# Sums for the down products on GpSimd's queue, a buffer of its own for the mean's weights, six places for the weight halves

## The chip, the cores and the metric

The kernel runs on one core of a Trainium2 chip. The metric is the device time of one execution in microseconds. Before the change it is 1877.29 us, the median of three runs (1876.36 to 1880.88).

## The reference

One layer of a decoder trunk is computed for a prompt of 1024 tokens and for eight sample tokens, 1032 columns in all, at a width of 1024, in float32. A combined projection feeds three branches (a gated linear recurrence, attention in a sliding window, attention into a memory of 256 tokens). Their outputs are gated, merged and projected, and then come a layer norm, a gated feed-forward part of width 2816 and a second layer norm:

```python
h = layer_norm(ALPHA * x + merged @ w_out, ln1_g, ln1_b)
gt, up = jnp.split(h @ w_gate_up, 2, axis=-1)
h = layer_norm(ALPHA * h + (jax.nn.silu(gt) * up) @ w_down, ln2_g, ln2_b)
```

The change bears on the feed-forward part: `h @ w_gate_up` (44 tiles of 128 output rows) and the product with `w_down` (8 tiles of 128 output rows over 22 tiles of input).

## The kernel before, in words

All data lie with the 128 rows of a tile on the partitions and the 1032 columns in the free dimension. A matrix product in float32 is made of three products in a rounded format: each operand is cut into a high half, written by ScalarE (L84), and a low half, the remainder, written by VectorE (L85), and the products high times high, high times low and low times high are summed in a bank of PSUM (matmuls in L332 to L334).

The large products save matmuls with seven products in place of eight for a two by two block scheme (Strassen's scheme in Winograd's form). A unit is a pair of weight tiles; step `i` of a unit (0 to 6) multiplies a weight block, or a sum of blocks, with a block or a sum of blocks of the columns. `fast_quarter` forms what a step needs of the weights: for some steps a sum by VectorE (L306), then the two halves. `fast_step` issues its 24 matmuls and takes the result out of PSUM.

The gate/up stage (`gate_up_down`, about 1230 to 1630 us in the trace) runs twenty gate/up units, of which eighteen go in nine pairs `u`, `v`; in a pair some of the products are themselves split again by the same scheme (steps named `p0` to `p6` and `v0` to `v6`, formed in `second_quarter` and `fifth_quarter`, run in `second_step` with matmuls in L1525 to L1527 and in `fifth_step` with L1465 to L1467). Eight units of the down product follow. The list `order` holds all steps. At each step the loop forms the weights of the step that is `ahead` = 3 places later, and then issues the step itself.

The weight halves have their places in `half_pair`: five for high halves (tag `qh`) and, in this stage, five for low halves (four with tag `ql` in one pool, every fifth in another). A half may be written when the matmuls that read its place's last content are done.

In step 0 of `v`, VectorE adds a bank of the split product (`pd`) to a partial sum (L389 in `fast_step`). The second product written to that bank, by the matmul at L1525 in step `p4`, has to wait for this reading.

For the down product the column operands are blocks of the gated activations, spilled to `scr_f` in HBM by `FinishGate` (L2059), and four sums of such blocks. `down_sums` forms the sums ahead of time, once for each of the two parts of the down product and twice in each part (`p` = 0, 1): three blocks are loaded (L1548 in `down_block`, 516 KB each), two differences are taken (L1563, L1565) and stored to `scr_t` (L1558 in `keep`), a fourth block is loaded and two more sums are formed and stored (L1570, L1573). All these DMAs are issued from SyncE's queue, which also issues the loads of raw weights (L265), the operands of the split products (L1417) and the spills. The blocks lie in z slots: eight buffers of 1032 columns, handed out in turn (`zt`) and given back (`zfree`), that the results of the units use too.

`weight_means` forms, for the mean of the second layer norm, the sums of the last six input tiles of `w_down`: eight loads of 384 KB (L1775) into a z slot, each followed by a reduction on VectorE (L1777), one load or reduction at every step 0 and 4.

Within the queues of the engines a planner orders the instructions by the order in which the program lists them and by the times at which it expects their inputs; an instruction that waits holds up all those behind it in its queue. Pools of SBUF memory are opened and closed by stage. `cst` and `sm` stay open to the end.

Of the kernel before, what the change touches and what calls it, by code (L numbers as in the profile page):

```python
# [19 lines left out]
P = 128  # L20
D = 1024
KT = D // P
TP = 1024
NB = 8
# [16 lines left out]
QN = T // 4  # L41
# [19 lines left out]
class Builder:  # L61
# [338 lines left out]
    def project(self, ctx, pool):  # L400

        nc, io, tc = self.nc, self.io, self.tc
        self.qdc = self.cst.tile([P, KT * NB], F32, name="qdc")
        self.qds = self.cst.tile([P, KT * NB], F32, name="qds")
        self.kd = self.cst.tile([P, 2 * NB], F32, name="kd")
        self.vd = self.cst.tile([NB, 256], F32, name="vd")
# [15 lines left out]
        ahead = 3  # L422
# [219 lines left out]
    def mem_scores(self, h, half, q, mk, between):  # L642

        nc = self.nc
        out = []
        for pr in range(2):
            s = self.bank("s", f"cs{h}_{half}_{pr}")
            for u in range(2):
                qt = pr * 2 + u
                self.mm3(s[:, u * 256:(u + 1) * 256], [  # L650
                    ((q[j][0][:, qt * P:(qt + 1) * P], q[j][1][:, qt * P:(qt + 1) * P]), mk[j]) for j in range(2)
                ])
            st = self.sm.tile([P, 8], F32, tag="cst", name=f"cst{h}_{half}_{pr}", bufs=4)
            p = self.ph.tile([P, 4 * 129], F32, tag="p", name=f"cp{h}_{half}_{pr}", bufs=4)[:, :512]
            nc.vector.tensor_reduce(st[:, 0:2], s.rearrange("p (a b) -> p a b", b=256), axis=AX.X,
                                    op=ALU.max, negate=True)
            for u in range(2):
                nc.scalar.activation(p[:, u * 256:(u + 1) * 256], s[:, u * 256:(u + 1) * 256], AF.Exp,
                                     bias=st[:, u:u + 1], scale=1.0, accum_out=st[:, 2 + u:3 + u])
            nc.vector.reciprocal(st[:, 4:6], st[:, 2:4])  # L660
            for u in range(2):
                nc.vector.tensor_scalar_mul(p[:, u * 256:(u + 1) * 256], p[:, u * 256:(u + 1) * 256],
                                            st[:, 4 + u:5 + u])
            out.append(p)
            if pr == 0:
                between()
        return out
# [108 lines left out]
    def win_scores(self, kv, ops, b, between=lambda: None):  # L776
# [7 lines left out]
        st = self.sm.tile([P, 12], F32, tag="bst", name=f"bst{kv}_{b}", bufs=4)  # L784
# [127 lines left out]
    def lru_consts(self):  # L912
# [3 lines left out]
        w = self.cst.tile([P, 8 * KT], F32, name="lruc")  # L916
# [3 lines left out]
        self.nsnk = self.cst.tile([P, 16], F32, name="nsnk")  # L920
        nc.vector.tensor_scalar_mul(self.nsnk, self.vec[:, V_SNK:V_SNK + 16], -1.0)
        self.hbg = self.cst.tile([P, 24], F32, name="hbg")
# [18 lines left out]
        self.sp4n = self.cst.tile([P, KT], F32, name="sp4n")  # L941
        nc.vector.tensor_scalar_mul(self.sp4n, t, -4.0)

    def lru_setup(self):
        self.scv = self.cst.tile([P, KT, 3, NB], F32, name="scv")
        self.scvo = self.cst.tile([P, KT, 3, NB], F32, name="scvo")
        self.sh = self.cst.tile([P, KT, NB], F32, name="sh")
        self.sho = self.cst.tile([P, KT, NB], F32, name="sho")
        self.pconv = self.cst.tile([P, KT, 3], F32, name="pconv")
        self.pho = self.cst.tile([P, KT], F32, name="pho")  # L950
# [84 lines left out]
    def dec_rows(self, qd, m0, dr, name):  # L1035

        nc = self.nc
        rows = self.sm.tile([NB, 256], F32, tag="drow", name=f"drow_{name}{m0}", bufs=1)
        ps = self.bank("o", f"drt_{name}{m0}")
        for i in range(2):  # L1040
            nc.tensor.transpose(ps[:NB, i * P:(i + 1) * P], qd[:, (m0 + i) * NB:(m0 + i + 1) * NB], self.ident)
        nc.scalar.copy(rows, ps[:NB, :256])
        nc.sync.dma_start(dr, rows)

    def dec_mem(self, h):
# [46 lines left out]
        st = self.sm.tile([P, 8], F32, tag="cst", name=f"dcst{h}", bufs=4)  # L1092
# [32 lines left out]
    def dec_win(self):  # L1125
# [9 lines left out]
        work = self.sm.tile([P, 256], F32, tag="drow", name="dwork", bufs=1)  # L1135
# [31 lines left out]
        st = self.sm.tile([P, 8], F32, tag="cst", name="dsst", bufs=4)  # L1167
# [10 lines left out]
        own = self.sm.tile([P, 8], F32, tag="cst", name="down", bufs=4)  # L1178
# [365 lines left out]
    def down_block(self, part, kh, th, p):  # L1544

        t = self.zt(f"f{part}{kh}{th}{p}")
        f0, t0 = 8 * part + 4 * kh, HT * th + QN * p
        self.nc.sync.dma_start(t.rearrange("p (k n) -> p k n", k=4), self.scr["f"][:, f0:f0 + 4, t0:t0 + QN])  # L1548
        return t

    def down_sums(self, part):


        tt = self.nc.vector.tensor_tensor
        for p in range(2):

            def keep(i, t):
                self.nc.sync.dma_start(self.scr["t"][:, part, p, (1, 2, 4, 6).index(i), :], t)  # L1558
# [4 lines left out]
            tt(b22, b22, b12, ALU.subtract)  # L1563
            keep(4, b22)
            tt(b12, b11, b12, ALU.subtract)  # L1565
# [34 lines left out]
    def gate_up_down(self, ts):  # L1600
# [29 lines left out]
        ahead = 3  # L1630
# [137 lines left out]
    def weight_means(self):  # L1768
# [3 lines left out]
        for m in range(KT):  # L1772
            z = self.zt(f"wsum{m}")
            raw = z[:, :nf * P]
            nc.sync.dma_start(raw, self.io["wdn"][m][:, f0 * P:(f0 + nf) * P])  # L1775
            yield
            nc.vector.tensor_reduce(part[:, m, :], raw.rearrange("p (k n) -> p k n", k=nf), axis=AX.X, op=ALU.add)  # L1777
            self.zfree(z)
            yield
# [183 lines left out]
    def build(self):  # L1963
# [8 lines left out]
        self.cdec = self.cst.tile([P, KT, NB], F32, name="cdec")  # L1972
# [12 lines left out]
        with ExitStack() as right:  # L1985
            slots = right.enter_context(ExitStack())
            self.slots = [slots.enter_context(pool("slots0", "right"))]
            with pool("acc") as acc, pool("gp") as self.gp:
# [23 lines left out]
                with pool("slots1") as slots1:  # L2012
# [212 lines left out]
```

## Time and profile before

| | |
|---|---|
| time, median of 3 runs | 1877.29 us (1876.36 to 1880.88) |
| time of the profiled execution | 1878.54 us |
| span of its instructions | 1876.8 us |
| TensorE (PE) busy | 1857.2 us, 99% of the span |
| VectorE (DVE) busy | 1441.6 us, 77% |
| ScalarE (ACT) busy | 1055.0 us, 56% |
| GpSimd (POOL) busy | 123.3 us, 7% |
| moved by DMA | 326.93 MB, 174 GB/s on average |

An instruction's row in a timeline gives its start and its duration in us, the engine, the line of the kernel, the operation, what it writes and reads by the program's names, and in brackets how long the engine was idle before it and what ended that. SP is SyncE; SPq rows are DMAs that it issues. A row of a line's instructions gives the shortest, median and longest duration in ns and the first and last start. Rows of waits give who waited for whom, the total in us, how many times and the longest.

### The profile page before, as it was taken

The page shows a single profiled execution, that of the slowest core. Times are in us where ns is not written, and L with a number is a line of the kernel's source. Part 1 is how long each engine was busy: PE and PEld are TensorE (multiplying, and loading weights), DVE is VectorE, ACT ScalarE, POOL GpSimd, SP SyncE. Part 2 cuts the span into 40 slices and gives each one's busy share as a digit, 9 for nine tenths or more (in the row PEclk, how much of TensorE's full clock was granted, in tenths as well). Part 3 has the DMA queues.
Part 4 walks back from the last instruction along what each step waited for, and adds up shares of the span by engine and source line. Part 5 has one row for each costly group of instructions (what it writes and reads, how often), then busy time and mean ns, then how long its engine had stood idle before and what let it go on. Part 6 is the DMA issues. An engine that isn't in the chain of part 4 may idle for free. (4 is left out here: it accounts for less than half of the span.)

```text
span 1876.8 us, 38124 instructions
## 1 busy us (share of the span) xinstructions
PE 1857.2 (99%) x14616; PEld 1839.9 (98%) x14616; DVE 1441.6 (77%) x2932; ACT 1055.0 (56%) x2250; POOL 123.3 (7%) x187
## 2 busy tenths in 40 slices
PE   9999999999999999999999999999999999999998
PEld 9999999999999999999999999999999999999998
DVE  7878878888789757568787567798787787857486
ACT  6576676665666756568774234544444434735355
POOL 1000002110000000021210000000000000001100
PEclk9999999999999999999999999999999999999999
DMA  9535345447344358647536251245586467866962
GB/s 337 171 115 175 110 143 168 137 139 263 119 160 168 121 195 272 212 128 238 173 99 190 91 192 57 69 167 183 183 272 205 154 216 246 262 169 188 206 184 91
DMA packets 186678, 326.93 MB, mean 174 GB/s; under 512 B 19760, under 2 KB 97536, under 8 KB 186496
## 3 DMA queue, kind: packets, MB, share of 16 engines
q1 hardware_dynamic: 179392, 304.86, 49.2%
q0 software_dynamic: 4224, 14.78, 3.9%
q10 hardware_dynamic: 2880, 4.85, 0.7%
q8 instruction: 115, 1.88, 0.4%
q14 instruction: 67, 0.55, 0.1%
HBM read 238.76 MB, written 89.84 MB: 175 GB/s over the span
## 5 line engine op out<-in xcount | busy, mean ns | idle before, releaser
L332 PE MATMUL ub<-th,u_6h 128*128 128x258 f32 x240 | 68.5, 285 | 1.3 <-DVE zb L380 0.6
L332 PE MATMUL ub<-th,u_2h 128*128 128x258 f32 x240 | 68.2, 284 | 0.9 <-ACT p1s L373 0.9
L332 PE MATMUL uc<-th,u_3h 128*128 128x258 f32 x240 | 68.1, 284 | 0.5 <-ACT v L503 0.5
L332 PE MATMUL ub<-th,u_4h 128*128 128x258 f32 x240 | 68.2, 284 | 0.2 <-ACT u2s L373 0.2
L332 PE MATMUL ud<-th,u_1h 128*128 128x258 f32 x240 | 68.1, 284 | 0.0
L334 PE MATMUL ud<-th,u_5l 128*128 128x258 f32 x240 | 68.1, 284 | 0.0
L332 PE MATMUL ud<-th,u_5h 128*128 128x258 f32 x240 | 68.1, 284 | 0.0
L332 PE MATMUL ub<-th,u_0h 128*128 128x258 f32 x240 | 68.1, 284 | 0.0
L334 PE MATMUL ub<-th,u_6l 128*128 128x258 f32 x240 | 68.1, 284 | 0.0
L334 PE MATMUL ub<-th,u_0l 128*128 128x258 f32 x240 | 68.1, 284 | 0.0
L334 PE MATMUL ud<-th,u_1l 128*128 128x258 f32 x240 | 68.1, 284 | 0.0
L334 PE MATMUL ub<-th,u_4l 128*128 128x258 f32 x240 | 68.1, 284 | 0.0
L334 PE MATMUL ub<-th,u_2l 128*128 128x258 f32 x240 | 68.1, 284 | 0.0
L334 PE MATMUL uc<-th,u_3l 128*128 128x258 f32 x240 | 68.0, 283 | 0.0
L333 PE MATMUL ub<-tl,u_6h 128*128 128x258 f32 x240 | 67.7, 282 | 0.0
L333 PE MATMUL ub<-tl,u_0h 128*128 128x258 f32 x240 | 67.7, 282 | 0.0
L333 PE MATMUL ud<-tl,u_5h 128*128 128x258 f32 x240 | 67.6, 282 | 0.0
L333 PE MATMUL ub<-tl,u_4h 128*128 128x258 f32 x240 | 67.6, 282 | 0.0
L333 PE MATMUL ud<-tl,u_1h 128*128 128x258 f32 x240 | 67.6, 282 | 0.0
L333 PE MATMUL ub<-tl,u_2h 128*128 128x258 f32 x240 | 67.6, 282 | 0.0
L333 PE MATMUL uc<-tl,u_3h 128*128 128x258 f32 x240 | 67.6, 282 | 0.0
L134 PE MATMUL op<-mh,woh 128*128 128x258 f32 x224 | 63.4, 283 | 0.0
(1080 smaller groups left out, 8228.8 us busy)
## 6 DMA issues: line engine op xcount, KB each, us to landing
ur<-win SPq DMA_DIRECT2D x120, 256.0 KB, 3.1
raw<-wgu SPq DMA_DIRECT2D x80, 256.0 KB, 3.5
t<-scr_t SPq DMA_DIRECT2D x36, 516.0 KB, 4.8
z<-scr_f SPq DMA_DIRECT2D x28, 516.0 KB, 4.8
scr_f<-z SPq DMA_DIRECT2D x22, 516.0 KB, 2.8
scr_t<-z SPq DMA_DIRECT2D x20, 516.0 KB, 3.2
raw<-wdn SPq DMA_DIRECT2D x35, 256.0 KB, 4.7
z<-scr_t SPq DMA_DIRECT2D x16, 516.0 KB, 8.8
```

Source lines behind the costliest of these rows:

```text
L134: nc.tensor.matmul(ps, sh, mh, start=opens and i == 0, stop=False)
L332: mm(sh[:, w], xh, start=opens and k == 0, stop=False)
L333: mm(sh[:, w], xl, start=False, stop=False)
L334: self.last_mm = mm(sl[:, w], xh, start=False, stop=k == 3).ins
```

## The change

The diff makes five edits.

- In the gate/up and down stage, high and low halves have six places each instead of five. The added places lie in the pool `w1`.
- The weights of a step are formed four steps ahead instead of three.
- In `down_sums` the loads of the blocks and the stores of the sums are issued from GpSimd's queue instead of SyncE's.
- `weight_means` loads into a buffer of its own in `w1` instead of a z slot, in sixteen pieces of 192 KB instead of eight of 384 KB, with sixteen reductions.
- Small tiles that only the first stages use (states, softmax columns and the like) move from `cst` and `sm` to a new pool `early`, which is closed before the pool `zf` of the out projection and the gate/up stage is opened. This gives the memory for the places and the buffer. No instruction on these tiles changes.

```diff
     def half_pair(self, name):
-        low = partial(self.wpool.tile, tag="ql", bufs=4)
+        high, low = (partial(self.wpool.tile, tag=f"q{e}", bufs=n) for e, n in (("h", 5), ("l", 4)))
         if self.sfree is not None:
             self.lows += 1
-            if self.lows % 5 == 0:
-                low = partial(self.w1.tile, tag="ql", bufs=1)
-        return self.wpool.tile([P, D // 2], F32R, tag="qh", name=f"{name}h", bufs=5), low([P, D // 2], F32R, name=f"{name}l")
+            if self.lows % 6 > 3:
+                low = partial(self.w1.tile, tag="ql", bufs=2)
+            if self.lows % 6 == 5:
+                high = partial(self.w1.tile, tag="qh", bufs=1)
+        return high([P, D // 2], F32R, name=f"{name}h"), low([P, D // 2], F32R, name=f"{name}l")
...
-    def down_block(self, part, kh, th, p):
+    def down_block(self, part, kh, th, p, queue=None):
...
-        self.nc.sync.dma_start(t.rearrange("p (k n) -> p k n", k=4), self.scr["f"][:, f0:f0 + 4, t0:t0 + QN])
+        (queue or self.nc.sync).dma_start(t.rearrange("p (k n) -> p k n", k=4), self.scr["f"][:, f0:f0 + 4, t0:t0 + QN])
...
     def down_sums(self, part):
-        tt = self.nc.vector.tensor_tensor
+        tt, other = self.nc.vector.tensor_tensor, self.nc.gpsimd
         for p in range(2):
             def keep(i, t):
-                self.nc.sync.dma_start(self.scr["t"][:, part, p, (1, 2, 4, 6).index(i), :], t)
-            b11, b12 = (self.down_block(part, 0, th, p) for th in range(2))
-            b22 = self.down_block(part, 1, 1, p)
+                other.dma_start(self.scr["t"][:, part, p, (1, 2, 4, 6).index(i), :], t)
+            b11, b12 = (self.down_block(part, 0, th, p, other) for th in range(2))
+            b22 = self.down_block(part, 1, 1, p, other)
...
-            b21 = self.down_block(part, 1, 0, p)
+            b21 = self.down_block(part, 1, 0, p, other)
...
-        ahead = 3
+        ahead = 4
...
-        for m in range(KT):
-            z = self.zt(f"wsum{m}")
-            raw = z[:, :nf * P]
-            nc.sync.dma_start(raw, self.io["wdn"][m][:, f0 * P:(f0 + nf) * P])
+        n = nf // 2
+        for m, e in ((m, e) for m in range(KT) for e in range(2)):
+            raw = self.w1.tile([P, n * P], F32, tag="wsum", name=f"wsum{m}_{e}", bufs=1)
+            nc.sync.dma_start(raw, self.io["wdn"][m][:, (f0 + e * n) * P:(f0 + (e + 1) * n) * P])
             yield
-            nc.vector.tensor_reduce(part[:, m, :], raw.rearrange("p (k n) -> p k n", k=nf), axis=AX.X, op=ALU.add)
-            self.zfree(z)
+            nc.vector.tensor_reduce(part[:, m, e * n:(e + 1) * n], raw.rearrange("p (k n) -> p k n", k=n), axis=AX.X,
+                                    op=ALU.add)
             yield
...
+        first = ExitStack()
+        self.early = first.enter_context(pool("early"))
+        self.cdec = self.early.tile([P, KT, NB], F32, name="cdec")
...
+            first.close()
             with pool("zf") as self.z:
```

More of the change, by code (lines that the diff above doesn't have):

```diff
@@ L402, in project @@
         nc, io, tc = self.nc, self.io, self.tc
[L403 to L406, printed above, removed]
+        self.qdc = self.early.tile([P, KT * NB], F32, name="qdc")
+        self.qds = self.early.tile([P, KT * NB], F32, name="qds")
+        self.kd = self.early.tile([P, 2 * NB], F32, name="kd")
+        self.vd = self.early.tile([NB, 256], F32, name="vd")
         self.lru_setup()
@@ L652, in mem_scores @@
                 ])
-            st = self.sm.tile([P, 8], F32, tag="cst", name=f"cst{h}_{half}_{pr}", bufs=4)
+            st = self.early.tile([P, 8], F32, tag="cst", name=f"cst{h}_{half}_{pr}", bufs=4)
             p = self.ph.tile([P, 4 * 129], F32, tag="p", name=f"cp{h}_{half}_{pr}", bufs=4)[:, :512]
@@ L783, in win_scores @@
         snk = self.nsnk[:, 4 * kv:4 * kv + 4]
-        st = self.sm.tile([P, 12], F32, tag="bst", name=f"bst{kv}_{b}", bufs=4)
+        st = self.early.tile([P, 12], F32, tag="bst", name=f"bst{kv}_{b}", bufs=4)
         p = self.ph.tile([P, 4 * 129], F32, tag="p", name=f"bp{kv}_{b}", bufs=4).rearrange("p (g n) -> p g n", g=4)
@@ L915, in lru_consts @@
         lam = self.vec[:, V_LAM:V_LAM + KT]
-        w = self.cst.tile([P, 8 * KT], F32, name="lruc")
+        w = self.early.tile([P, 8 * KT], F32, name="lruc")
         self.sp2 = w[:, 0:8]
@@ L919, in lru_consts @@
         e, z, z2, acc, t = (w[:, 24 + 8 * i:32 + 8 * i] for i in range(5))
-        self.nsnk = self.cst.tile([P, 16], F32, name="nsnk")
+        self.nsnk = self.early.tile([P, 16], F32, name="nsnk")
         nc.vector.tensor_scalar_mul(self.nsnk, self.vec[:, V_SNK:V_SNK + 16], -1.0)
-        self.hbg = self.cst.tile([P, 24], F32, name="hbg")
+        self.hbg = self.early.tile([P, 24], F32, name="hbg")
         nc.vector.tensor_scalar_mul(self.hbg, self.vec[:, V_BG:V_BG + 24], 0.5)
@@ L940, in lru_consts @@
         nc.vector.tensor_scalar_mul(self.sp2, t, 2.0)
-        self.sp4n = self.cst.tile([P, KT], F32, name="sp4n")
+        self.sp4n = self.early.tile([P, KT], F32, name="sp4n")
         nc.vector.tensor_scalar_mul(self.sp4n, t, -4.0)
     def lru_setup(self):
[L945 to L950, printed above, removed]
+        self.scv = self.early.tile([P, KT, 3, NB], F32, name="scv")
+        self.scvo = self.early.tile([P, KT, 3, NB], F32, name="scvo")
+        self.sh = self.early.tile([P, KT, NB], F32, name="sh")
+        self.sho = self.early.tile([P, KT, NB], F32, name="sho")
+        self.pconv = self.early.tile([P, KT, 3], F32, name="pconv")
+        self.pho = self.early.tile([P, KT], F32, name="pho")
     def load_lru(self):
@@ L1037, in dec_rows @@
         nc = self.nc
-        rows = self.sm.tile([NB, 256], F32, tag="drow", name=f"drow_{name}{m0}", bufs=1)
+        rows = self.early.tile([NB, 256], F32, tag="drow", name=f"drow_{name}{m0}", bufs=1)
         ps = self.bank("o", f"drt_{name}{m0}")
@@ L1091, in dec_mem @@
         pr = ph.tile([NB, 256], F32, tag="dp", name=f"dcp{h}", bufs=1)
-        st = self.sm.tile([P, 8], F32, tag="cst", name=f"dcst{h}", bufs=4)
+        st = self.early.tile([P, 8], F32, tag="cst", name=f"dcst{h}", bufs=4)
         nc.vector.tensor_reduce(st[:NB, 0:1], ps[:NB, :256], axis=AX.X, op=ALU.max, negate=True)
@@ L1134, in dec_win @@
             nc.sync.dma_start(io[name][:, P - 1, :], row)
-        work = self.sm.tile([P, 256], F32, tag="drow", name="dwork", bufs=1)
+        work = self.early.tile([P, 256], F32, tag="drow", name="dwork", bufs=1)
         qb, sc = work[:, :P], work[:, P:]
@@ L1166, in dec_win @@
         pr = qb
-        st = self.sm.tile([P, 8], F32, tag="cst", name="dsst", bufs=4)
+        st = self.early.tile([P, 8], F32, tag="cst", name="dsst", bufs=4)
         snk = self.vec[:, V_SNKD:V_SNKD + 1]
@@ L1177, in dec_win @@
         nc.vector.tensor_scalar_mul(sc, self.ident, pr[:, 0:1])
-        own = self.sm.tile([P, 8], F32, tag="cst", name="down", bufs=4)
+        own = self.early.tile([P, 8], F32, tag="cst", name="down", bufs=4)
         nc.vector.tensor_reduce(own, self.ident.rearrange("p (b r) -> p b r", b=NB), axis=AX.X, op=ALU.add)
```

1 line of the change is left out of this document (removed).

## The prediction

> **What bounds the kernel now.** I read the busy times first, then the granted clock by stage, then the waits of the matmul engine, then the engines' timelines around those waits.
>
> ```profile
> span 1876.8 us, 38124 instructions
> PE 1857.2 (99%) x14616; PEld 1839.9 (98%) x14616; DVE 1441.6 (77%) x2932; ACT 1055.0 (56%) x2250; POOL 123.3 (7%) x187
> ```
> ```profile
> 1200.00:1400.00 200.00, 199.50 (x1652) 198.91 (x1651) 173.36 (x309) 93.71 (x175) 0.00 (x0) 1.00 0.57 188
> 1400.00:1450.00 50.00, 48.23 (x401) 48.03 (x401) 40.06 (x76) 19.18 (x38) 0.00 (x0) 1.00 0.70 233
> ...
> 1500.00:1550.00 50.00, 49.11 (x408) 48.91 (x408) 40.65 (x78) 19.77 (x39) 0.00 (x0) 1.00 0.66 217
> 1550.00:1600.00 50.00, 48.24 (x398) 47.85 (x397) 41.23 (x72) 22.71 (x45) 0.00 (x0) 1.00 0.74 241
> 1600.00:1850.00 250.00, 250.00 (x2081) 249.87 (x2080) 173.82 (x290) 127.47 (x247) 20.85 (x24) 1.00 0.69 190
> ```
>
> The second fence is a table by stretch: span, then busy time of PE, PEld, DVE, ACT and POOL, granted clock, DMA share, GB/s. PE is busy for 1857.2 of 1876.8 us at a full clock, so all its waits together are 19.6 us. The diff changes the work of the gate/up stage and a few tiles' homes; in that stage PE idles only between 1400 and 1600 us, and from 1600 to 1850 not at all. The waits of PE from 1090 to 1800 us (total, times, longest):
>
> ```profile
> PE pdfg L1525 <- DVE p1sfg L389: 3.6, 3, 1.8
> PE qbfg L1465 <- DMA t<-scr_t: 0.8, 1, 0.8
> ```
>
> So 3.6 + 0.8 = 4.4 us is about all that the edits can win: 0.23% of the time. The matmul at L1525 that writes the bank "pd" may not start until VectorE has read that bank in L389. Without other work L389 comes just in time:
>
> ```profile
> 1292.64 0.69 DVE L85 TENSOR_TENSOR ufg_2l<-s,ufg_2h 128x512 fp32r<-128x512 f32 x1 [2.67 <-ACT ufg_2h L84]
> ...
> 1295.49 0.69 DVE L85 TENSOR_TENSOR ufg_v0l<-s,ufg_v0h 128x512 fp32r<-128x512 f32 x1 [0.51 <-ACT ufg_v0h L84]
> 1296.10 0.42 DVE L389 SCALAR_TENSOR_TENSOR p1sfg<-pdfg,p1sfg 128x258 f32<-128x258 f32 x1
> ...
> 1296.57 0.38 PE L1525 MATMUL pdfg<-hh,ufg_p4h 128*128 128x258 f32 x1
> ```
>
> L389 ends at 1296.10 + 0.42 = 1296.52 and PE goes on at 1296.57. VectorE stood idle for 2.67 us shortly before, for a high half that ScalarE had not yet cut. At the longest stall the sums for the down products come in between:
>
> ```profile
> 1401.39 0.32 SPq L2059 DMA_DIRECT2D scr_f<-z  x1
> 1401.77 0.42 SPq L1548 DMA_DIRECT2D z<-scr_f  x1
> ...
> 1405.08 0.37 SPq L1548 DMA_DIRECT2D z<-scr_f  x1
> ...
> 1412.74 2.07 SPq L1558 DMA_DIRECT2D scr_t<-z  x2
> ```
> ```profile
> 1407.14 0.42 DVE L85 TENSOR_TENSOR ufg_p6l<-raw,ufg_p6h 128x256 fp32r<-128x256 f32 x1
> 1411.48 1.23 DVE L1563 TENSOR_TENSOR z<-z,z 128x1032 f32<-128x1032 f32 x1 [3.92 <-DMA z<-scr_f]
> 1412.63 0.69 DVE L85 TENSOR_TENSOR ufg_2l<-s,ufg_2h 128x512 fp32r<-128x512 f32 x1
> 1413.23 1.23 DVE L1565 TENSOR_TENSOR z<-z,z 128x1032 f32<-128x1032 f32 x1
> 1414.38 0.68 DVE L306 TENSOR_TENSOR s<-s,raw 128x512 f32<-128x512 f32 x1
> 1414.98 0.68 DVE L85 TENSOR_TENSOR ufg_v0l<-s,ufg_v0h 128x512 fp32r<-128x512 f32 x1
> 1415.58 0.42 DVE L389 SCALAR_TENSOR_TENSOR p1sfg<-pdfg,p1sfg 128x258 f32<-128x258 f32 x1
> 1416.06 0.39 PE L1525 MATMUL pdfg<-hh,ufg_p4h 128*128 128x258 f32 x1 [1.77 <-DVE p1sfg L389]
> ```
>
> VectorE's queue is in order. L1563, the first sum, stands in it ahead of its data: the block loaded at 1405.08 lands some 6.4 us later, VectorE idles 3.92 us, and then five operations (1411.48 to 1415.58, 4.10 us) run before L389. PE loses 1.77 us. The other two stalls are of the same kind, with less waiting:
>
> ```profile
> 1528.28 1.23 DVE L1563 TENSOR_TENSOR z<-z,z 128x1032 f32<-128x1032 f32 x1 [1.50 <-DMA z<-scr_f]
> ...
> 1534.67 0.38 PE L1525 MATMUL pdfg<-hh,ufg_p4h 128*128 128x258 f32 x1 [0.89 <-DVE p1sfg L389]
> 1570.05 1.23 DVE L1563 TENSOR_TENSOR z<-z,z 128x1032 f32<-128x1032 f32 x1 [3.08 <-DMA z<-scr_f]
> ...
> 1574.63 0.39 PE L1525 MATMUL pdfg<-hh,ufg_p4h 128*128 128x258 f32 x1 [0.92 <-DVE p1sfg L389]
> ```
>
> 1.77 + 0.89 + 0.92 = 3.58 us.
>
> ```profile
> L389 DVE SCALAR_TENSOR_TENSOR p1sfg<-pdfg,p1sfg x9: 418/419/423, 1256.5 to 1574.1; 128x258 f32<-128x258 f32 x9
> ...
> L1563 DVE TENSOR_TENSOR z<-z,z x4: 1226/1232/1233, 1372.3 to 1570.0; 128x1032 f32<-128x1032 f32 x4
> ```
>
> L389 runs nine times, L1563 four times. The first L1563, at 1372.3, stands behind the forming operations, waits for nothing and costs PE nothing that the waits show.
>
> **Part 1: six places, four steps ahead.** No instruction is added: a low and a high half get one place more, and each step's weights are formed one step earlier. What that is worth is read from the three stalls. At 1411.48 the path from data to L389 holds three forming operations (ufg_2l, L306, ufg_v0l) at about 0.60 us from start to start, 1.80 us. VectorE was idle for 3.92 us just before; if these three already lie there, the path is 4.10 - 1.80 = 2.30 us and the stall of 1.77 is gone. The same 1.2 to 1.8 us would cover 0.89 and 0.92. That is the upper end, a gain of 3.58 us. The lower end is 0: with everything one step earlier, the operations of the step after may move into the vacated place, since the planner fills VectorE's queue by the times it expects, and the number of operations per step is the same. I see no row that decides between the ends, and take the middle: 1.8 us won. Where the idle stretch that gave cover is gone (the 2.67 us above is spent by then), each forming operation that ends up in front of L389 costs 0.60 us; this is a rival below.
>
> **Part 2: the sums' DMAs on GpSimd's queue.** Sixteen block loads (L1548 inside the sums) and sixteen stores (L1558) leave SyncE's queue. No other work of GpSimd is queued there at that time: the table above shows POOL at 0.00 until 1600. What they cost there is bounded by the nearest rows:
>
> ```profile
> L1548 SPq DMA_DIRECT2D z<-scr_f x28: 370/378/951, 1338.1 to 1701.0; - x28
> ...
> DMA to landing us min/median/max: 3.6/4.8/6.2
> ```
> ```profile
> L1766 POOL DMA_DIRECT2D z<-scr_h x7: 866/878/886, 1739.9 to 1789.9; - x7
> ...
> DMA to landing us min/median/max: 5.5/6.5/10.0
> ```
> ```profile
> L538 POOL DMA_DIRECT2D scr_mk<-mkr x8: 539/540/705, 12.8 to 34.0; - x8
> ```
>
> A 516 KB load from GpSimd's queue takes 0.88 us to issue and 6.5 us to land, against 0.38 and 4.8 from SyncE's: 1.7 us later, with ends of 5.5 - 6.2 = -0.7 and 10.0 - 3.6 = +6.4. It doesn't start sooner in return: the block at 1405.08 waits for a free z slot, which the store issued at 1401.39 still reads (SyncE's own waits, below), and that store keeps its queue. What SyncE's queue gains (it stands at L1558 until 1412.74, with weight loads behind it) is hidden already, since no wait of PE names a weight load.
>
> ```profile
> SPq L1548 <- DMA scr_f<-z: 7.1, 4, 1.8
> ```
>
> So lateness of L1563's data by 1.7 us at four places is 6.8 us on VectorE at most; nothing if the planner puts L1563 behind L389, where the forming operations then cover it. I take 0.5 us lost, near the lower end, because the gain in part 1 is only counted by half and the room left there takes most of the delay. The 0.83 us at qbfg is a load behind SyncE's other transfers; one 516 KB store fewer among them gives 0 to 0.8, and I take 0.2 won.
>
> The Trainium skill, page "DMA: Bandwidth & Descriptors", section "Issuing engines are not separate DMA queues", says that DMAs from any engine run on the same 16 DMA engines and that another issuer only saves the time of issuing. By that rule part 2 wins nothing by itself; the trace agrees as far as SyncE's 0.38 us is no bottleneck. The skill's page "SBUF — State Buffer", section "A bandwidth-pool intuition that's wrong", tells of a DMA from GpSimd's queue that took about 3100 ns instead of 620 beside a VectorE copy, which holds a port that GpSimd needs; its section "Who interferes with whom" says that a tensor_tensor, which is what VectorE runs here, was not seen to do so. No issue in the rows above shows that loss; by the page's larger figure every load would issue some 2.5 us later, and the result would be that of rival B.
>
> **Part 3: the mean's weights in a buffer of their own.**
>
> ```profile
> L1777 DVE TENSOR_REDUCE wpart<-z x8: 942/943/947, 1251.7 to 1384.7; 128x6 f32<-128x768 f32 x8
> ...
> L1775 SPq DMA_DIRECT2D z<-wdn x8: 328/404/631, 1229.8 to 1380.5; - x8
> ```
>
> Eight reductions of 0.94 us become sixteen of half the width. From 0.69 us at 512 columns (L85) and 0.42 at 256 the fixed part is about 0.15, so one takes (0.94 - 0.15)/2 + 0.15 = 0.55 and all 8.8 instead of 7.5 us. The 1.3 us more fall into VectorE's idle time (about 10 us in each 50); uncovered, one in front of L389 at each of the three stalls would be 1.6 us. Eight more issues on SyncE are 8 x 0.40 = 3.2 us of a queue that mostly waits. With twice as many steps the reductions last to about 1229.8 + 2 x 154.9 = 1540 us instead of 1385, far ahead of the last products. One z slot more is free until 1385 us, ahead of all three stalls. The tiles that move to the early pool keep their instructions; its memory is reused long after their last use. I take 0 for all of it.
>
> **The sum.** -1.8 + 0.5 - 0.2 = -1.5 us. The profiled execution took 1878.54 us, 1.74 around its span, and would come to 1877.0; against the median of 1877.29 that is 1875.8 us.
>
> **The rivals.** A: the full gain. Forming moves out of the way and the landing doesn't matter: -4.4, 1872.9 us. For it speaks that the idle 3.92 and 3.08 us hold 1.8 us easily; against it the later landing in part 2.
>
> B, the slower side: the block loads are dear on GpSimd's queue. The POOL rows above move 128 whole rows each, while a block of scr_f is 512 runs of 1032 bytes. If issuing goes by runs, a load takes up to 4 x 0.88 = 3.5 us. Where two loads follow each other (two of the four sums) the data is 7.0 - 0.9 = 6.1 us later, at the other two 3.5 - 0.4 = 3.1, together 18.4 us. Less 1.8 us of cover at four places that leaves 11.2: 1888.5 us. Against it: 0.54 us for a 128 KB store of 128 short rows and 0.88 for long ones show that the count of runs isn't all. It decides from an issue of about 1.8 us on.
>
> C: the planner does something else with the freedom: one forming operation more stands in front of L389 in each of the nine pairs of units, 9 x 0.60 = 5.4 us, 1882.7 us. The rows at 1296 show that L389 has no slack; that per step the count stays the same speaks against it.
>
> D: the edits cancel or move nothing, 1877.3 us: the places aren't what PE waits for, and delay and room are of one size.
>
> **How the numbers follow.** Forecast 0.40, A 0.18, B 0.16, C 0.08, D 0.18. A measurement of this kernel tells about 0.3%, 5.6 us, from no change: faster is below 1871.7, slower above 1882.9. The forecast, D and nearly all of A lie between. A's upper tail gives faster 0.05; most of B and half of C give slower 0.17; 0.78 is left for no change. The range goes from 1871.5, a little past all known waits removed, to 1884.0, past C and into the mild part of B.
>
> **What would show it.** Right: the wait of pdfg for L389 falls from 3.6 to around 2 us while PE's busy time stays at 1857; ufg_2l and L306 stand ahead of L1563; a load from GpSimd's queue issues in about 0.9 us and lands after 6 to 7. Wrong: POOL issues of 2 us and more, and waits of VectorE for scr_f above 8.5 us in total (B); a pdfg wait in all nine pairs (C); or PE waits that are new, such as one for a weight half.

## The result, and the profile after the change

The changed kernel takes 1896.77 us (median of four runs, 1895.52 to 1898.79) against 1876.95 for the kernel before beside it: a ratio of 1.0102, with a 95% interval of 1.0085 to 1.0120. It is slower by 1%. The profiled execution has a span of 1897.1 us, 20.3 more than before. From L120 on, the lines of the changed kernel stand two lines later: L389 is now L391, L1525 is L1527, L1548 is L1550, L1558 is L1560, L1563 to L1573 are L1565 to L1575, L1777 is L1779; the spill L2059 is L2064, the product before it L2063.

Three views of the page first: busy times, and the two groups of DMAs that moved, with their size and the median us from issue to landing.

```profile
span 1897.1 us, 38165 instructions
PE 1862.0 (98%) x14616; PEld 1844.9 (97%) x14616; DVE 1440.5 (76%) x2940; ACT 1055.2 (56%) x2250; POOL 144.9 (8%) x219
...
z<-scr_f POOLq DMA_DIRECT2D x16, 516.0 KB, 5.3
scr_t<-z POOLq DMA_DIRECT2D x16, 516.0 KB, 3.4
```

VectorE does the same work. PE's busy time grew by 4.8 us for the same 14616 matmuls, so some matmuls ran longer. The table by stretch, whose columns are as in the prediction, shows where:

```profile
1400.00:1450.00 50.00, 40.26 (x310) 39.83 (x310) 34.74 (x68) 15.62 (x30) 4.45 (x7) 0.90 0.58 199
1500.00:1550.00 50.00, 47.47 (x393) 47.06 (x392) 37.87 (x73) 19.59 (x39) 4.34 (x7) 1.00 0.57 187
1550.00:1600.00 50.00, 43.88 (x346) 43.67 (x345) 36.09 (x67) 18.96 (x36) 5.02 (x8) 0.93 0.66 221
1600.00:1850.00 250.00, 249.79 (x2076) 249.48 (x2076) 172.13 (x297) 125.11 (x245) 20.61 (x24) 1.00 0.73 199
```

The loss lies around 1420 and 1590 us: 310 matmuls in place of 401, 346 in place of 398, and a granted clock of 0.90 and 0.93 in place of 1.00. PE's waits, and VectorE's for the block loads, name the cause of the idle part:

```profile
PE pdfg L1527 <- DVE p1sfg L391: 17.4, 4, 8.8
PE ubfg L334 <- DVE z L369: 1.0, 1, 1.0
...
DVE z L1565 <- DMA z<-scr_f: 13.1, 3, 6.0
```

In the kernel before, the last of these was:

```profile
DVE z L1563 <- DMA z<-scr_f: 8.5, 3, 3.9
```

The wait for L391 grew from 3.6 to 17.4 us; it is the wait that the change could have shortened. At its longest place VectorE did this:

```profile
1412.43 0.69 DVE L308 TENSOR_TENSOR s<-s,raw 128x512 f32<-128x512 f32 x1
1418.94 1.23 DVE L1565 TENSOR_TENSOR z<-z,z 128x1032 f32<-128x1032 f32 x1 [5.82 <-DMA z<-scr_f]
...
1421.57 0.68 DVE L85 TENSOR_TENSOR ufg_v0l<-s,ufg_v0h 128x512 fp32r<-128x512 f32 x1
...
1422.51 1.23 DVE L1572 TENSOR_TENSOR z<-z,z 128x1032 f32<-128x1032 f32 x1
1423.65 0.69 DVE L85 TENSOR_TENSOR ufg_4l<-s,ufg_4h 128x512 fp32r<-128x512 f32 x1
1424.25 0.42 DVE L391 SCALAR_TENSOR_TENSOR p1sfg<-pdfg,p1sfg 128x258 f32<-128x258 f32 x1
```

The first sum starts 7.5 us later than before (1418.94 against 1411.48), and 5.31 us lie between it and L391 where there were 4.10, because the third sum (L1572) now stands ahead of L391 too. Why the data comes late is seen in GpSimd's timeline:

```profile
1399.96 0.77 POOL L1550 DMA_DIRECT2D z<-scr_f  x1 [12.13 <-DVE z L2063]
1408.12 0.78 POOL L1550 DMA_DIRECT2D z<-scr_f  x1 [7.39 <-DVE ufg_p6l L85]
1413.91 0.75 POOL L1550 DMA_DIRECT2D z<-scr_f  x1 [5.01 <-DMA z<-scr_f]
```

in its waits:

```profile
POOL z L1550 <- DMA z<-scr_f: 15.5, 3, 5.4
```

and in the durations of L1550, shortest, median and longest, with the landings below:

```profile
L1550 POOL DMA_DIRECT2D z<-scr_f x14: 751/768/782, 1367.0 to 1582.7; - x14
...
DMA to landing us min/median/max: 4.2/5.2/7.8
```

A load issues in 0.77 us, which is cheap. But the next one starts only when the last has landed: the first takes the 7.8 us of this row and lands at 1407.79, the second starts 0.33 us later. Three of GpSimd's waits (15.5 us) name an earlier block load, although the program has no wait of one block load for another. For the second load the profile names VectorE's L85 instead, which was done about 0.5 us before; that it too waited for the first load's landing is shown by the runs with more descriptor memory, below.

The clock is the second part of the loss. PE's timeline at the stall's end:

```profile
1424.73 0.58 PE L1527 MATMUL pdfg<-hh,ufg_p4h 128*128 128x258 f32 x1 [8.77 <-DVE p1sfg L391]
```

and two windows right behind it, columns as above:

```profile
1424.70:1430.30 5.60, 5.57 (x26) 5.57 (x27) 3.54 (x8) 1.89 (x4) 0.00 (x0) 0.50 0.24 97
1430.30:1436.00 5.70, 5.70 (x47) 5.70 (x47) 5.03 (x10) 1.86 (x3) 0.53 (x1) 0.95 0.41 137
```

For 5.6 us after the stall the granted clock is 0.50 and a matmul takes 5.57 / 26 = 0.214 us, then 5.70 / 47 = 0.121. From start to start, 28 matmuls run at that pace here and 24 behind the stall of 6.1 us at 1592.8: 2.8 + 2.4 = 5.2 us. Together: 13.8 us more waiting for L391, 1.0 for the new wait of ubfg, 0.8 less for qbfg, 5.2 for the clock, 19.2 of 20.3 us.

### The profile page after: what moved, and what is told of

Its sections match the earlier page's. It is cut to its first block, busy times and chain, and to the rows that moved or that the text cites. A ratio compares the mean times of both kernels' runs of the same rounds, so it can differ in the third digit from the quotient of the medians.

```text
span 1897.1 us, 38165 instructions
## 1 busy us (share of the span) xinstructions
PE 1862.0 (98%) x14616; PEld 1844.9 (97%) x14616; DVE 1440.5 (76%) x2940; ACT 1055.2 (56%) x2250; POOL 144.9 (8%) x219
## 3 DMA queue, kind: packets, MB, share of 16 engines
q8 instruction: 115, 1.88, 0.4%
```

## The experiments

Ratios are to the kernel before on the same chip, with 95% intervals. "Wait" is PE's wait for L391 (L389) in the profile.

| run | us | ratio | wait, us |
|---|---|---|---|
| the change | 1896.77 | 1.0102 (1.0085 to 1.0120) | 17.4 |
| qonly | 1903.39 | 1.0130 (1.0114 to 1.0147) | 23.8 |
| sp | 1881.52 | 1.0013 (1.0003 to 1.0022) | 3.1 |
| loadsp | 1883.01 | 1.0017 (1.0007 to 1.0026) | 4.0 |
| places | 1877.19 | 0.9992 (0.9983 to 1.0001) | 4.1 |
| mean | 1876.90 | 0.9993 (0.9980 to 1.0005) | 3.7 |
| ring1088 | 1892.44 | 1.0074 (1.0057 to 1.0092) | 11.7 |
| ring1344 | 1890.15 | 1.0062 (1.0044 to 1.0079) | 10.9 |
| rows | 1893.13 | 1.0075 (1.0060 to 1.0090) | 7.5 |
| quiet | 1895.80 | 1.0088 (1.0067 to 1.0108) | 15.7 |
| late2 | 1890.61 | 1.0056 (1.0036 to 1.0077) | 10.4 |
| spill | 1902.04 | 1.0118 (1.0100 to 1.0137) | 17.8 |
| both | 1902.45 | 1.0121 (1.0095 to 1.0146) | 16.0 |
| echo | 1892.45 | 1.0069 (1.0052 to 1.0085) | 13.5 |
| hold | 1874.69 | 0.9981 (0.9970 to 0.9991) | none |
| places_hold | 1876.10 | 0.9981 (0.9971 to 0.9991) | 0.6 |
| sp_hold | 1875.35 | 0.9981 (0.9971 to 0.9990) | 0.8 |
| ahold | 1882.68 | 1.0022 (1.0009 to 1.0034) | 5.6 |
| holdnomean | 1880.68 | 1.0009 (1.0000 to 1.0019) | none |

**Which part costs the time.** `qonly` is the kernel before with the queue alone, `sp` the whole change without the queue. `places` and `mean` are the kernel before with part 1 or part 3 alone (and the memory of the early pool), on SyncE's queue.

```diff
-        tt, other = self.nc.vector.tensor_tensor, self.nc.gpsimd
+        tt, other = self.nc.vector.tensor_tensor, self.nc.sync      # sp
```

> The kernel before with that part alone: the sums' loads and stores on GpSimd's queue; five places, three steps ahead, mean in z slots. Theory Q: the loads of one sum go one after another, each starting about 0.3 us after the landing of the one before, VectorE waits 10 us and more for them in total, pdfg waits 10 to 18 us and the clock drops behind a long wait; 1887 to 1897 us. Rival P: within 2 us of the kernel before.

> The changed kernel with one part undone: the sums' loads and stores are issued from SyncE's queue again; six places, four steps ahead and the mean's buffer stay. Theory Q (the loss is the queue: on GpSimd each block load starts only when the load before it has landed): the four long or middling waits of pdfg shrink to those of the kernel before or less, the PE clock stays full; 1873 to 1879 us. Rival P (the loss comes from forming a step earlier, which puts more of VectorE's work in front of L391): the waits stay, 1885 us and more.

> The kernel before with part 1 alone: six places for high and low halves, weights formed four steps ahead; the sums' DMAs on SyncE's queue, the mean's weights in z slots as before. The prediction's step (1.8 us won, ends 0 and 3.6): 1876 to 1878.5, against 1878.5 of the kernel before in these runs, with the wait for pdfg at 1 to 3 us. Rival (the planner fills the vacated places with other work, so that nothing or less than nothing is won): 1878.5 to 1881, wait for pdfg 3.5 us or more.

> The kernel before with part 3 alone: the mean's weights in one buffer of their own in sixteen pieces. The prediction's step: nothing, 1878.5. Theory M (with one buffer each reduction stands in VectorE's queue for a load that could only start after the last reduction, and this goes on beyond 1400 us where the sums are): waits of wpart for wsum of 8 us or more on VectorE and 1880 to 1883.

The queue carries the loss: without it 1881.5 us, with it alone 1903.4, more than with the whole change. Theory Q has the side right in both runs and the size wrong: `sp` came out above its 1879, `qonly` above its 1897. `qonly` is not late data alone. In its trace all four sums stand ahead of L389 at all four places, where the kernel before has the third and fourth ahead at one place only (near 1531 us), so VectorE's order changed as well. By the ratios the other parts together win back about 5 us when the loads are late, with intervals that just overlap. By themselves, the places and the buffer win nothing that can be told from no change (both intervals hold 1), and on SyncE's queue together they cost 0.13%. In `sp` VectorE stands for the mean's one buffer:

```profile
PE pdfg L1527 <- DVE p1sfg L391: 3.1, 3, 1.8
...
DVE wpart L1779 <- DMA wsum<-wdn: 7.5, 4, 2.9
```

In `mean` alone no such wait of VectorE shows after 1330 us, so theory M fell for that run. In `places` the time lies in the expected range, but the wait is 4.1 us and not 1 to 3, which is the rival's sign. `loadsp` leaves only the sixteen stores on GpSimd's queue:

```diff
-            b11, b12 = (self.down_block(part, 0, th, p, other) for th in range(2))
-            b22 = self.down_block(part, 1, 1, p, other)
+            b11, b12 = (self.down_block(part, 0, th, p) for th in range(2))
+            b22 = self.down_block(part, 1, 1, p)
...
-            b21 = self.down_block(part, 1, 0, p, other)
+            b21 = self.down_block(part, 1, 0, p)
```

> The kernel after with the sixteen block loads issued from SyncE again and the sixteen stores left on GpSimd's queue. If the loads alone carry the loss (Q): 1880 to 1883, waits for pdfg about 3 us. If the stores on GpSimd's queue have a part in it: above 1886, with a store standing in front of something that PE waits for.

With 1883.0 against 1881.5 us for `sp` the stores cost little or nothing, and the loads nearly all.

**Why one load waits for another.** Two runs give GpSimd's DMAs more descriptor memory. The order of the work on all engines stays that of the changed kernel.

```diff
-    nc = bacc.Bacc("TRN2", target_bir_lowering=False, num_devices=1, dynamic_dma_scratch_size=1024)
+    nc = bacc.Bacc("TRN2", target_bir_lowering=False, num_devices=1, dynamic_dma_scratch_size=1088)   # ring1344: 1344
```

> The changed kernel with one number changed, the SBUF set aside for GpSimd's DMAs: 1088 bytes a partition instead of 1024; the order on every engine is the same. Theory Q, with the reason that one block load of 512 runs fills more than half of that space (512 runs over 16 engines and one more each, 33 of 64 places of 16 bytes; 68 places hold two): two block loads are under way together, the third of a sum starts without waiting for the second to land where its slot is free, the data of the first sum comes about 5 us earlier, pdfg waits 2 to 7 us instead of 17.4, no clock drop; 1878 to 1886 us. Rival G (GpSimd's loads are late for another reason, such as issuing, its port or the DMA engines' load): 1895 to 1898 us, as before this edit.

> The same with 1344 bytes (84 places of 16 bytes: two loads of 33, not three). Theory Q: as with 1088, within 1.5 us of it. Rival S (every byte of that space helps, by smooth degrees): clearly faster than 1088. Rival G: 1895 to 1898 us.

The timeline of GpSimd in `ring1344`:

```profile
1400.89 0.77 POOL L1550 DMA_DIRECT2D z<-scr_f  x1 [12.49 <-DVE z L2063]
1404.58 0.77 POOL L1550 DMA_DIRECT2D z<-scr_f  x1 [2.92 <-DVE z L369]
1411.14 0.76 POOL L1550 DMA_DIRECT2D z<-scr_f  x1 [5.80 <-DMA scr_f<-z]
```

and PE's wait there:

```profile
PE pdfg L1527 <- DVE p1sfg L391: 10.9, 3, 5.1
```

The second load now starts as soon as its z slot is free, 4 us before the first has landed, and no wait of GpSimd for a block load is left, with 1088 bytes as with 1344. So the loads went one after another for want of descriptor memory; that is shown. By the medians it is worth 4.3 us with 1088 bytes and 6.6 with 1344; the intervals don't tell these two apart. The Trainium skill, page "DMA: Bandwidth & Descriptors", section "SWDGE vs HWDGE vs iDMA", says that a DMA issued from GpSimd puts its descriptors into rings in SBUF; under "Terms" it gives 16 bytes a descriptor, and under "The descriptor swizzle" 9 an engine for 128 rows. An estimate from these: 512 runs take 512 / 16 + 1 = 33 places, two loads 66, or 1056 bytes; 1024 is just too little and 1088 enough. The runs agree.

But the time was expected to fall to 1878 to 1886 us, and it stays 9 us above `sp`. `rows` looks from another side, with a quarter of the runs in each load and the descriptor memory as it was. It reads other blocks than the sums need, so it computes another result; only its times count.

```diff
-        (queue or self.nc.sync).dma_start(t.rearrange("p (k n) -> p k n", k=4), self.scr["f"][:, f0:f0 + 4, t0:t0 + QN])
+            queue.dma_start(t, self.scr["f"][:, f0 + 2 * th + p, :])
```

> The kernel after, but each block load of the sums on GpSimd's queue reads one whole row set of scr_f (128 runs of 4128 B in place of 512 of 1032 B, the same 516 KB); the sums are therefore formed of other activations. Theory Q (a load of 512 runs fills most of GpSimd's descriptor space, so the next load starts only when the last has landed): with a quarter of the runs two loads fit, the second is issued within 1 us of its cause and not 0.3 us after a landing, the waits for pdfg fall from 17.4 us to under 5, and the time is 1880 to 1884, that of the kernel after with SyncE's queue (1881.5). Rival V (GpSimd's queue as such is slow, or VectorE's order alone decides): the waits stay above 10 us and the time is 1890 or more.

The block loads of `rows` (its L1553), shortest, median and longest issue and landing:

```profile
L1553 POOL DMA_DIRECT2D z<-scr_f x14: 527/532/542, 1361.3 to 1579.4; - x14
...
DMA to landing us min/median/max: 3.9/6.2/8.0
```

A load issues in 0.53 in place of 0.77 us and no load waits for another, as theory Q said. Yet a load still takes 6.2 us to land, PE waits 7.5 us for L391 and 5.1 for a bank that VectorE reads at L382, and the time is 1893.1, where theory Q had 1880 to 1884: neither the runs nor the descriptor memory makes up the rest.

**What makes the rest.** With room for two loads, the third one waits for the z slot that a spill gives back, and the spill issued at 1404.19 lands only at 1410.70, 6.5 us later, which releases GpSimd's row at 1411.14 above. SyncE's row of that spill in `ring1344`:

```profile
1404.19 0.32 SPq L2064 DMA_DIRECT2D scr_f<-z  x1
```

In `sp` the same spill takes 4.2 us, to 1406.27, and the third load follows at once:

```profile
1402.08 0.32 SPq L2064 DMA_DIRECT2D scr_f<-z  x1
...
1406.34 0.37 SPq L1550 DMA_DIRECT2D z<-scr_f  x1
```

At this place the path from the first sum to L391 is also longer, 5.31 us in `ring1344` against 3.91 in `sp`, because L1572 stands in it. The spill's 2.3 us and the path's 1.4 cover the 3.3 us by which the stall is longer (5.1 against 1.8). Four runs looked for what makes this. `quiet` takes the mean's loads and the copies of the caches away from SyncE's queue at that time, `late2` lists the third and fourth sum behind L391, `spill` issues the spills from GpSimd's queue too, `both` joins the last two.

```diff
-                    for _ in range(2):
-                        next(copies, None)                          # quiet, with weight_means as before
...
-            tt(b11, b11, b22, ALU.add)
+            with self.tc.issue_after(self.pd_read):                 # late2: up to the second store
+                tt(b11, b11, b22, ALU.add)
...
-        nc.sync.dma_start(b.scr["f"][:, self.f, :], za)
+        nc.gpsimd.dma_start(b.scr["f"][:, self.f, :], za)           # spill
```

> The kernel after with room for two loads in GpSimd's descriptor space (1344 bytes), the mean's weights as in the kernel before, and the copies of the caches (L1297, L1299) moved behind the stage. Theory T (on SyncE's queue the copies and the mean's loads stood behind the wait for a z slot; without it they run beside the block loads, make them and the spill land late, and hold VectorE): the spill lands in 4 us in place of 6.5, waits for pdfg under 5 us, 1878 to 1884. Rival L (loads from GpSimd's queue are late of themselves): waits of 9 us and more, 1887 to 1891 as with the larger space alone (1890.2).

> The kernel after with room for two loads, and with the third and fourth sum (L1572, L1575) behind L391 in VectorE's queue; the first two sums stay ahead of it, loads on GpSimd's queue. Theory V (of each large stall 1.2 us is the third sum standing ahead of L391, and stalls over 4 us cost as much again in clock): the two large stalls shrink from 5.1 and 4.1 us to about 3.8 and 2.8 us, no matmuls at half the clock behind them, 1884 to 1887 against 1890.2. Rival: the place is taken by other work and the waits stay at 10 us, 1889 to 1891.

> The kernel after with room for two loads (descriptor space 1344 bytes) and with the spills of the gated activations (L2064) issued from GpSimd's queue too, ahead of the block loads. Theory F (the spill that gives back the z slot of the third block shares the DMA engines with block loads of the other queue, and so lands in 6.5 us in place of 4.2; in one queue the transfers are served in their order): the spill lands in 4 to 4.5 us at the two places where it is waited for, the third load starts some 2 us sooner there, waits for pdfg 6 to 9 us in place of 10.9, 1884 to 1888. Rival L (GpSimd's DMAs are slow of themselves): the spill lands in 6 us or more, 1889 to 1893.

> The two edits of the runs beside this one together: spills on GpSimd's queue, third and fourth sum behind L391, room for two loads. If F and V each hold and add up: waits for pdfg of 3 to 5 us and 1879 to 1883, as with SyncE's queue (1881.5). If one of them is wrong: 1885 or more.

Theories T, V and F all fell. `quiet` took 1895.8 us, not 1878 to 1884: with the mean's weights back in z slots a stall of 5 us appears in the pair at 1384 us, where the kernel with the buffer of its own has none, and a block load at 1413.66 takes 7.9 us and the spill issued at 1413.28 takes 6.7 us although the copies are gone. In `late2` the third sum did move behind L391, but the longest stall stayed at 5.1 us and the time at 1890.6, as its rival said. `spill` and `both` are the slowest of the four. The spills of `spill`, all on GpSimd's queue, land no sooner:

```profile
L2064 POOL DMA_DIRECT2D scr_f<-z x15: 532/532/564, 1360.5 to 1637.5; - x15
...
DMA to landing us min/median/max: 3.7/5.3/7.6
```

Their median is 5.3 us, against 4.0 for those on SyncE's queue in `ring1344`. The run doesn't show that GpSimd's queue is slow whatever goes through it. At 1415.59 a block load there again waits 4.5 us for an earlier one; spills and loads now share the descriptor memory, which may be why. And the stores that the change moved land in 3.4 us, against 3.2 on SyncE's queue before. `echo` asks whether that queue is slow of itself or the two queues take engine time from each other. It is `places`, all on SyncE's queue, plus sixteen copies on GpSimd's queue that nobody reads; VectorE's order is the same.

```diff
         nc.sync.dma_start(b.scr["f"][:, self.f, :], za)
+        if self.f < 16:
+            nc.gpsimd.dma_start(b.scr["d"][:, self.f, :], b.scr["f"][:, self.f, :])
```

> The kernel with part 1 alone on SyncE's queue (run places, 1877.2), and beside it, on GpSimd's queue, one more copy in HBM of each of the first sixteen spilled rows of activations (516 KB each, 8.3 MB in all as in the kernel after, read by nobody), each issued when its spill has landed. The order of all other engines' work is that of run places. Theory S (a second queue takes its share of the sixteen DMA engines, so that transfers on SyncE's queue that the sums wait for land later): block loads and their spills land 1 us or more later, the waits for pdfg grow from 4 to 7 us or more, 1880 to 1886. Rival L (GpSimd's transfers are slow of themselves and disturb nobody): 1876 to 1878.5.

It took 1892.5 us, more than theory S expected. At the sums near 1410 us in `places`, the third load's issue on SyncE:

```profile
1404.79 0.37 SPq L1550 DMA_DIRECT2D z<-scr_f  x1
```

the first sum on VectorE:

```profile
1410.80 1.23 DVE L1565 TENSOR_TENSOR z<-z,z 128x1032 f32<-128x1032 f32 x1 [1.33 <-DMA z<-scr_f]
```

and the queue's packets, MB and share of the sixteen engines between the two:

```profile
q1 hardware_dynamic: 1531, 2.07, 102.2%
```

The same three in `echo`:

```profile
1405.84 0.37 SPq L1550 DMA_DIRECT2D z<-scr_f  x1
```
```profile
1413.55 1.23 DVE L1565 TENSOR_TENSOR z<-z,z 128x1032 f32<-128x1032 f32 x1 [3.30 <-DMA z<-scr_f]
```
```profile
q1 hardware_dynamic: 1342, 1.76, 64.4%
q0 software_dynamic: 288, 1.06, 38.2%
```

In `places` SyncE's queue (q1) has all of the engines and the third load's sum starts 6.0 us after the load's issue. In `echo` the other queue (q0) takes 38% and the same step lasts 7.7 us. The engines are full in both, and a load that is waited for lands later while the other queue takes its share. The spill ahead of it lands nearly as soon, after 3.9 us against 3.6 in `places`. In `ring1344`, between 1404 and 1416 us, the engines are shared in the same way:

```profile
q1 hardware_dynamic: 1291, 2.48, 57.8%
q0 software_dynamic: 402, 1.46, 37.1%
```

The Trainium skill, same page, section "Queues, rings and completion order", says that each DMA engine goes round robin between the queues that it has work for, packet by packet. These shares agree with it as far as both queues are served at once; they don't test the turn by packets. `echo` also moves 8.3 MB more, copied within HBM, so it shows that traffic on a second queue delays the sums and that the stalls follow, not what a second queue does to the same bytes. Whether the share alone, at equal bytes, makes the 7 to 9 us between `ring1344` and `loadsp` or `sp`, and why the spill takes 6.5 us, stays open.

**The order of the sums.** `hold` is the kernel before with one edit, which keeps the sums behind L389 in VectorE's queue. `places_hold` adds part 1, `sp_hold` all but the queue. `ahold` is the whole change with that edit, `holdnomean` the same with the mean's weights as before.

```diff
-            if (i in (2, 4) and where[u] % 2 == 0 or i == 0 and where[u] % 2) and sums and next(sums[0], self) is self:
-                sums.popleft()
+            if (i in (2, 4) and where[u] % 2 == 0 or i == 0 and where[u] % 2) and sums:
+                with self.tc.issue_after(self.pd_read):             # pd_read: the instruction of L389 (L391)
+                    if next(sums[0], self) is self:
+                        sums.popleft()
```

> The kernel before with the same edit of the order (sums behind L389), nothing else. H: the three stalls of 3.6 us go, 1873 to 1875.5 against 1877 of the kernel before. Rival Z: the sums then stand in front of the next step's forming operations and a wait for a weight half (ufg) of the same size appears, 1876 to 1880.

> The kernel before with part 1 (six places, four steps ahead) and with all sums behind L391 in VectorE's queue; DMAs on SyncE's queue, the mean's weights as before. If the two gains add up: 1872 to 1874 against 1878.5 of before, 1 to 2 us better than the sums behind L389 alone (1874.7). If the places win only what the sums' order wins as well: 1874 to 1876.

> The whole change with the sums' DMAs on SyncE's queue and the sums behind L391 in VectorE's queue. If the order of the sums removes all that is left of the stalls: 1873 to 1876, as the two other kernels with that order (1874.7 and 1876.1). If the mean's reductions, which here go on beyond 1400 us and wait for their one buffer, now hold L391 up: 1877 to 1881.

> The kernel after with one edit of the order: the sums of the down products are listed to stand behind L391 in VectorE's queue, so that they can wait for their loads without holding L391 up. The loads stay on GpSimd's queue, one after another. Theory H (the loss is the sums' waiting ahead of L391, plus the lower clock after the idle of over 4 us): no wait for pdfg over 1 us, no lower clock, and 1875 to 1881, a gain of 16 to 21 us. Rival Z (the lateness only moves: forming operations behind the held sums, or z slots given back late, stop PE elsewhere): other waits of 5 us and more, 1885 to 1895.

> The kernel after with the sums behind L391 in VectorE's queue and with the mean's weights as in the kernel before; the sums' DMAs stay on GpSimd's queue, with its descriptor space as it was. Theory H+M (in the run with the sums behind L391 alone, the one stall left, 5.6 us, ended four reductions and a raw weight's wait): no wait for pdfg above 1 us, 1874 to 1878 against 1882.7. Rival: the stall comes from the raw weight (L1489) and stays, 1880 to 1884.

VectorE's timeline in `hold`:

```profile
1414.84 0.42 DVE L389 SCALAR_TENSOR_TENSOR p1sfg<-pdfg,p1sfg 128x258 f32<-128x258 f32 x1
1415.17 1.22 DVE L1563 TENSOR_TENSOR z<-z,z 128x1032 f32<-128x1032 f32 x1
```

and its engines by stretch:

```profile
1500.00:1550.00 50.00, 50.00 (x417) 49.95 (x416) 41.28 (x79) 20.30 (x40) 0.00 (x0) 1.00 0.59 198
1550.00:1600.00 50.00, 50.00 (x416) 49.94 (x415) 42.79 (x74) 24.05 (x45) 0.00 (x0) 1.00 0.79 269
```

The sum runs right behind L389 without waiting, the wait is gone, and the kernel is faster than the kernel before by 0.19%: 0.9981, with an interval clear of 1. Part 1 and part 3 add nothing to that. With the loads on GpSimd's queue the same edit brings 1896.8 down to 1882.7 us, and to 1880.7 with the mean's weights as before; theory H's 1875 to 1881 was a little too good for `ahold`. In `ahold` the one stall left at L391 stands behind a reduction that waits 3.7 us for the mean's buffer (VectorE waits 9.8 us for wsum in all). The execution that was profiled is the slowest of its ten, 1891.9 us where the others took 1880.5 to 1883.7, so that stall need not be in the others. In `holdnomean` the lateness moved, as rival Z of `ahold` said, to the next reading of a bank; its own theory's 1874 to 1878 fell. VectorE's timeline there:

```profile
1412.51 0.42 DVE L391 SCALAR_TENSOR_TENSOR p1sfg<-pdfg,p1sfg 128x258 f32<-128x258 f32 x1
1418.38 1.23 DVE L1565 TENSOR_TENSOR z<-z,z 128x1032 f32<-128x1032 f32 x1 [5.45 <-DMA z<-scr_f]
1419.54 0.42 DVE L1538 SCALAR_TENSOR_TENSOR z<-pbfg,p1sfg 128x258 f32<-128x258 f32 x1
```

and PE's wait:

```profile
PE pbfg L1527 <- DVE z L1538: 4.2, 1, 4.2
```

## Why the prediction was wrong

The forecast was 1875.8 us with a range to 1884.0; the time is 1896.8. What bounds the kernel was read rightly: the loss is at the wait and at the places that the prediction quoted, and `hold` wins about what those three stalls held (3.58 us; 0.19% of 1878.5 is 3.6).

**Part 2 is the step that failed.** It took 0.5 us for the lateness of L1563's data, out of 6.8 at most, which was 1.7 us, the difference of two median landings, at four places. It counted one load's landing each time. The runs show three loads in a row, each behind the landing of the last, and with that cured a spill that lands 2.3 us later (6.5 against 4.2) beside the traffic of two queues. At 1418.94 the data is 5.6 us late (7.46 less the 1.88 by which the spill ahead, at 1403.27 in place of 1401.39, is itself later). The step had written down +6.4 us as the far end of one load's lateness and then left it out of its most: 4 x 6.4 = 25.6 us. That this is near what `qonly` costs, 1.3% or 24 us, is chance: there the order and the clock have a part. The step also called what SyncE's queue gains hidden. Its copies now go out 0.4 us behind the spill (1403.64 after 1403.27) and not 4.1 (1405.51 after 1401.39), beside the transfers that are waited for. That this makes the spill late is not shown: in `quiet`, without them, it still took 6.7 us.

**The cover in part 2.** "The forming operations then cover it" did not hold: L1565 stayed ahead of L391 at all four places, and L1572 came ahead of it at three of them (1.23 us each). The third sum stands ahead at one place in the kernel before, at two in `places`, at three in `mean` and `sp` and at four in `qonly`; so several edits move it, and at the longest stall it is ahead in the changed kernel but not in `sp` (1418.36, after L391 at 1415.56).

**The clock was missing from the sum.** The working added stalls as idle time only. Long ones cost 5.2 us more, because of the drop to 0.50 behind them. The Trainium skill, page "TensorE: Matmul & The Clock Gate", section "What's actually happening", gives this rule: the clock halves after an idle window of about 3.4 us. The windows at 1424.70 and 1430.30 agree for a stall of 8.8 us. Five pauses of 1.95 to 3.3 us were followed by the lower clock too (last section), so 3.4 us is not a safe limit here.

**Part 1** was put at the middle, 1.8 us. In the stall the forming operations did move ahead (ufg_2l and L308 lie before 1413.1), but others took their place (in `places` L1432, L1433 and L1489), which was the lower end; the path from the first sum to L389 is 3.91 us in `places` (1410.80 to 1414.71) against 4.10. The wait there is 4.1 us, not "around 2". **Part 3** at 0 holds for `mean` alone; beside the other parts its waits cost VectorE 7.5 us in `sp` and hold up L391 in the profiled execution of `ahold`.

**The rivals.** B had the right side and the right object, and its 1888.5 was the nearest number, but that is luck, as its reason is wrong: an issue is 0.77 us, far below its 1.8, and the runs matter through descriptor memory. Of its signs, the waits of VectorE for scr_f did pass 8.5 us (13.1). C's sign, a wait in all nine pairs, did not come: there are four waits. The Trainium skill, page "DMA: Bandwidth & Descriptors", section "Issuing engines are not separate DMA queues", was weighed only for "wins nothing"; that transfers of two queues interleave on the same engines, which it also says, is what `echo` shows as a loss.

## What to carry to other kernels

Where the DMA engines are full, a second issuing queue adds no bandwidth and takes its share from the transfers that are waited for: in `echo` both queues together had 102.6% of the engines' time, in `places` one alone had 102.2%. Before moving loads to GpSimd's queue, count the descriptors of one load against the descriptor memory, and ask what happens with three loads in a row, not with one. And where a late operand stands ahead of an urgent operation in an engine's queue, change the order in that queue first: that alone won the whole 0.19% here, and it made the kernel indifferent to the places and the buffer, though not to the queue (1882.7 us against 1875.4).

## What the runs showed of the hardware that was not expected

- The halved clock after idle stretches, over all runs here. Of 39 pauses of PE from 0.6 to 1.95 us in the gate/up stage (start to start, less one matmul) none is followed by matmuls at 0.214 us; of 15 between 1.95 and 3.3 us 5 are; of 25 above 3.3 us all are. It costs 13 to 28 matmuls at that pace, 1.4 to 2.8 us. After some of the shorter pauses it sets in only some matmuls later. So a stall of 4 us costs 5.4 us or more.
- GpSimd takes 0.77 us to issue a load of 512 runs and 0.53 us for one of 128, but stands idle until the last load has landed, up to 5.4 us, when its descriptor memory holds only one of them. The profile shows this in three cases as idle time whose releaser is an earlier load, with no wait for it in the program.
- An isolated load on GpSimd's queue isn't slow: the shortest landings are 4.2 us there and 4.1 on SyncE's in `sp` (3.7 in the kernel before). Beside 1.7 MB of SyncE's transfers (the load at 1399.96) it takes 7.8.
